# Seven-product FFN on one core: norm in place, down-projection activations moved to the operand tiles, residual loads moved ahead of the last store

## The chip, the core and the metric

The kernel runs on one core of a Trainium2 chip. The metric is the device time of one execution in microseconds, the median of several runs. Five engines work side by side, each through its own queue in order: TensorE (PE, matmuls; its weight loads are listed as PEld), VectorE (DVE), ScalarE (ACT), GpSimd (POOL) and SyncE (SP, which here issues most of the DMAs). They pass work on through semaphores. Matmul results land in PSUM; everything else lies in SBUF.

## The reference, cut to what matters

The program is two residual layers on a 1024 x 1024 float32 stream x (tokens by features): a state-space mixer (ssd), a gated conv feed-forward block (FFN), differential attention (attn), and a second FFN. The change is in the FFN and in the hand-over into it:

```python
def conv_ffn(xn, up_w, conv_w, conv_b, down_w):      # D_MODEL 1024, D_FF 2816, FFN_CONV 3
    h = causal_dwconv(xn @ up_w, conv_w, conv_b)     # up: 1024 -> 2 * 2816
    a, b = h[..., :D_FF], h[..., D_FF:]
    return (silu(a) * b) @ down_w                    # down: 2816 -> 1024

x = x + conv_ffn(rmsnorm(x, norm_ffn_g), ...)
```

## The kernel before

**Layout and precision.** Features lie on the 128 partitions, tokens on the free axis. The residual is 16 SBUF tiles `xres[m, h]` of 128 x 512 floats (8 feature blocks m, 2 token halves h; in a trace `x`). Every float32 operand of a product is split in a high part (cast by ACT) and a low part (subtracted by DVE or POOL), and a product is three matmuls, high·high, high·low and low·high, each 128 x 128 by 128 x 512. `parts` (L805 to L808) splits activations, `split_weight` (L99 to L107) and `split` (L895 to L907) split weights: cast on ACT, low part on POOL (`wh`, `wl`).

**Norm (L205 to L252).** The mixer that ends before an FFN adds its result into `xres` and feeds squares to a `Norm`. `stats` turns the sums into a reciprocal root per token and copies it to a small tile `rkeep`; `apply` spreads it over a PSUM tile (`token_spread`, L185 to L194: small DVE products `dg`, then matmuls `rb`), scales x into a scratch tile `xnt` (L245), and splits that into `xn_h`, `xn_l` (`xh`, `xl` in a trace). x itself keeps the residual.

**Up half of an FFN (L788 to L962).** Weight blocks 0 to 3 (`PLAIN = 2` pairs) are multiplied in the plain way: 4 blocks x 2 halves x 24 matmuls = 192 (L860 to L870). The other 20 pairs of blocks go through a seven-product scheme (L933 to L961): a pair's weights and the normalised x are 2 x 2 quarters; with four sums of weight quarters (`sums`, L909 to L918) and four sums of x quarters (T1 to T4), seven products of 12 matmuls each, 84 a pair, stand for eight. PSUM tiles of a pair are `px`, `py`, `pz`, `pw`; ACT copies px out three times and DVE adds py, pz and pw. `pz` is used twice in a pair: the fourth product (pz<-t1) fills it, DVE reads it at L953, then the last product (pz<-xh) fills it again, and DVE adds that at L957.

`combine` (L831 to L855) makes T1 to T3 while the plain blocks run: it spreads both halves' roots again (4 `dg`, two `rb`), stores the residual to DRAM (`xm_d`, 16 DMAs), scales x again into `cv` scratch (16 products, L843), makes 16 differences (L847, L850, L852, L855) and splits them. The last difference goes into the tile of x, and T4 is split from it (L871 to L873).

`conv` (L810 to L826) runs once a pair: ACT applies the last tap, DVE the other two (L817), ACT the silu, DVE the product (L822), SP the store to DRAM (`a_d`). Pair 0's result is split on the chip instead (`pre`).

**Down half (L966 to L1018).** After the last pair the x tiles are allocated anew and loaded from `xm_d` (L966, the DMAs at L357). The 22 pairs are summed in groups, `FFN_GROUPS` = (0,1) (1,5) (5,9) (9,13) (13,16) (16,19) (19,22). `fetch` loads a group's stored results (`ad`) and splits them into `ah`, `al`, tiles of a pool of their own; `down` runs 48 wide matmuls per pair of blocks into `dp` (L118 to L120), and DVE adds each `dp` into x (L1002).

**What sets the order.** The framework's scheduler places instructions in each engine's queue by the program's order and by the memory that pools give back; DMAs of the residual and of `a_d` share SP's queue. `up.close()` and `wp.release()` (L961, L962) give back the memory of the up half.

## Time and profile before

| | us |
|---|---|
| median of 3 runs (lowest, highest) | 3100.83 (3097.57, 3105.54) |
| profiled execution, its own time | 3096.0 |
| its span, first to last instruction | 3094.3 |
| ssd, from 0 | to 877 |
| first FFN | 877 to 1612 |
| attention | to 2341 |
| second FFN | to 3094 |

| whole span | PE | PEld | DVE | ACT | POOL |
|---|---|---|---|---|---|
| busy us | 2866.7 | 2217.7 | 2117.1 | 1240.1 | 1334.3 |
| share | 93% | 72% | 68% | 40% | 43% |

The mean granted TensorE clock is 0.966 of full speed. A matmul's time in a row is from its start to its end in the pipeline, and matmuls overlap; what one costs is the distance from its start to the next start. In rows of waits, "PE px L924 <- ACT wh L903" is idle time of PE before matmuls into px that ended with ACT's cast of wh.

### The profile page before, as it was taken

How to read it: one execution, taken by the hardware profiler on the slowest of the kernel's cores; microseconds unless marked ns; L12 is line 12 of the kernel's file. 1: busy time of each engine (PE TensorE's matmuls, PEld its weight loads, DVE VectorE, ACT ScalarE, POOL GpSimd, SP SyncE). 2: the span in 40 equal slices, each digit the busy share in tenths (PEclk: the TensorE clock that was granted, in tenths of full speed). 3: DMA queues.
4: the chain of work that ended last, by engine and by line, in shares of the span. 5: the costliest groups of instructions: out<-in, count | busy, mean ns of one | idle time of the engine just before them, and what ended most of it. 6: DMA issues, size and time to landing. Idle time of an engine off the chain costs nothing.

```text
span 3094.3 us, 36239 instructions
## 1 busy us (share of the span) xinstructions
PE 2866.7 (93%) x13164; PEld 2217.7 (72%) x13164; DVE 2117.1 (68%) x3244; ACT 1240.1 (40%) x1973; POOL 1334.3 (43%) x892
## 2 busy tenths in 40 slices
PE   6999999989987999979998999999998799998999
PEld 4877777767775777767876666666676577776887
DVE  4646666677788777763357888888769877776333
ACT  4444444443334444432124555545444444443111
POOL 2245555547455444421235333333436544442222
PEclk8999999999998999989999999999999899999999
DMA  3445554555422222133332112111633222213323
GB/s 95 139 128 166 154 165 149 174 184 173 138 99 75 82 82 82 69 123 109 99 106 78 50 55 62 55 55 49 194 113 104 75 82 82 82 68 136 103 92 113
DMA packets 182979, 327.85 MB, mean 106 GB/s; under 512 B 20432, under 2 KB 88016, under 8 KB 182800
## 3 DMA queue, kind: packets, MB, share of 16 engines
q1 hardware_dynamic: 155536, 251.07, 24.7%
q10 hardware_dynamic: 18432, 58.73, 5.7%
q0 software_dynamic: 8832, 15.73, 2.1%
q8 instruction: 104, 1.70, 0.2%
q14 instruction: 75, 0.61, 0.1%
HBM read 240.99 MB, written 76.09 MB: 102 GB/s over the span
## 4 chain that ended last, share of the span: by engine, by line
PE 46%; DVE 32%; POOL 6%; issue 6%; ACT 5%; DMA 4%; SPq 0%; ACTq 0%; DVEq 0%; POOLq 0%
PE mm L293 6%; PE mm L294 6%; PE mm L295 6%; DVE cv L817 6%; PE dp L119 5%; PE dp L120 5%; PE dp L118 5%; PE pz L924 4%; DVE cv L822 4%; DVE sa L915 3%; POOL wl L904 3%; PE s L1310 2%; DVE cv L442 2%; DVE dg L190 1%; PE s L1309 1%
## 5 line engine op out<-in xcount | busy, mean ns | idle before, releaser
L105 POOL TENSOR_TENSOR wl<-ws,wh 128x1024 fp32r<-128x1024 f32 (+3 forms) x208 | 449.6, 2162 | 809.7 <-ACT wh L103 731.8
L293 PE MATMUL mm<-xh,wh 128*128 128x512 f32 x1280 | 543.7, 425 | 11.9 <-ACT xh L246 9.7
L294 PE MATMUL mm<-xl,wh 128*128 128x512 f32 x1280 | 510.7, 399 | 2.4 <-DVE xl L247 1.7
L295 PE MATMUL mm<-xh,wl 128*128 128x512 f32 x1280 | 510.3, 399 | 1.3 <-POOL wl L105 1.3
L103 ACT CAST wh<-ws 128x1024 fp32r<-128x1024 f32 (+3 forms) x208 | 192.5, 926 | 457.8 <-PE dp L119 248.8
L1002 DVE TENSOR_TENSOR x<-x,dp 128x512 f32<-128x512 f32 x224 | 151.9, 685 | 261.2 <-PE dp L120 247.9
L293 PEld LDWEIGHTS mm<-xh,wh 128*128 128x128 f32 x1280 | 247.7, 194 | 76.4 <-issue 18.1
L294 PEld LDWEIGHTS mm<-xl,wh 128*128 128x128 f32 x1280 | 247.1, 193 | 57.8 <-issue 8.4
L295 PEld LDWEIGHTS mm<-xh,wl 128*128 128x128 f32 x1280 | 245.6, 192 | 56.6 <-POOL wl L105 2.0
L119 PE MATMUL dp<-al,wh 128*128 128x512 f32 x672 | 266.0, 396 | 2.0 <-DVE al L808 1.8
L118 PE MATMUL dp<-ah,wh 128*128 128x512 f32 x672 | 264.3, 396 | 1.4 <-ACT ah L807 1.4
L120 PE MATMUL dp<-ah,wl 128*128 128x512 f32 x672 | 265.5, 395 | 0.0
L817 DVE SCALAR_TENSOR_TENSOR cv<-raw,fcw,cv 128x1024 f32<-128x1024 f32 x176 | 230.1, 1367 | 5.6 <-ACT cv L815 5.5
L442 DVE SCALAR_TENSOR_TENSOR cv<-raw,cw,cv 128x1024 f32<-128x1024 f32 x72 | 126.2, 1754 | 55.2 <-ACT cv L440 28.2
L1324 ACT ACTIVATE p<-s,nb,rq 128x256 f32<-128x256 f32 (+7 forms) x128 | 107.0, 836 | 114.9 <-DVE nb L1313 61.2
L119 PEld LDWEIGHTS dp<-al,wh 128*128 128x128 f32 x672 | 126.1, 188 | 33.9 <-DVE al L808 3.6
L118 PEld LDWEIGHTS dp<-ah,wh 128*128 128x128 f32 x672 | 125.9, 188 | 33.7 <-ACT ah L807 2.8
L120 PEld LDWEIGHTS dp<-ah,wl 128*128 128x128 f32 x672 | 126.1, 188 | 30.5
L904 POOL TENSOR_TENSOR wl<-sa,wh 128x1024 fp32r<-128x1024 f32 x40 | 97.3, 2434 | 109.3 <-ACT wh L903 104.6
L904 POOL TENSOR_TENSOR wl<-sc,wh 128x1024 fp32r<-128x1024 f32 x40 | 127.9, 3198 | 6.6 <-ACT wh L903 6.1
L904 POOL TENSOR_TENSOR wl<-ws,wh 128x1024 fp32r<-128x1024 f32 x40 | 103.6, 2590 | 29.9 <-ACT wh L903 29.9
L822 DVE TENSOR_TENSOR cv<-cv 128x1024 f32<-128x1024 f32 x44 | 114.8, 2610 | 0.4
(330 smaller groups left out, 6667.4 us busy)
## 6 DMA issues: line engine op xcount, KB each, us to landing
ws<-in_ffn_up_w_dram SPq DMA_DIRECT2D x96, 512.0 KB
a_d<-cv SPq DMA_DIRECT2D x42, 512.0 KB
ad<-a_d SPq DMA_DIRECT2D x42, 512.0 KB
ws<-in_ssd_in_w_dram ACTq DMA_DIRECT2D x40, 512.0 KB
seg<-acs_d SPq DMA_DIRECT2D x32, 512.0 KB
ws<-in_ssd_out_w_dram ACTq DMA_DIRECT2D x32, 512.0 KB
xbc_d<-cv SPq DMA_DIRECT2D x24, 512.0 KB
xc<-xbc_d SPq DMA_DIRECT2D x32, 384.0 KB
```

The costliest lines, as they stand in the source:

```text
L103: act.copy(wh[:, :n], ws[:, :n])
L105: pool.tensor_tensor(wl[:, :n], ws[:, :n], wh[:, :n], op=ALU.subtract)
L118: pe.matmul(ps, wh[:, m, k, :], xh, start=k == 0, stop=False)
L119: pe.matmul(ps, wh[:, m, k, :], xl, start=False, stop=False)
L120: pe.matmul(ps, wl[:, m, k, :], xh, start=False, stop=k == n - 1)
L293: pe.matmul(ps, wh[:, 0, k, :], xh, start=k == 0, stop=False)
L294: pe.matmul(ps, wh[:, 0, k, :], xl, start=False, stop=False)
L295: pe.matmul(ps, wl[:, 0, k, :], xh, start=False, stop=k == nk - 1)
L442: dve.scalar_tensor_tensor(cv, raw[:, 1 + k:1 + k + T], cw[:, i, k:k + 1], cv, op0=ALU.mult, op1=ALU.add)
L817: dve.scalar_tensor_tensor(cv, raws[b][:, 2 + k:2 + k + T], cw[:, n, k:k + 1], cv, op0=ALU.mult, op1=ALU.add)
L822: dve.tensor_tensor(cvs[1], cvs[0], cvs[1], op=ALU.mult)
L904: pool.tensor_tensor(wl, t, wh, op=ALU.subtract)
```

## The change

- **Norm in place.** `apply(in_place=True)` writes the scaled x into x itself, in all four hand-overs into an FFN (two per layer). The residual is stored to `xm_d` by the mixers, as each block is finished. `stats` no longer copies to `rkeep`.
- **Combine.** x now holds the normalised values, so the second spread of the roots and the 16 scalings go. Four differences per quarter block stay, in place. T1's low part is POOL's, T2's DVE's, T3's DVE's for even k and POOL's for odd (before: POOL's).
- **Starts.** The first seven-product pair's weights are loaded ahead of the last plain block; its a1 split stands ahead of the sums; conv 0 stands after plain block (1, 2), conv 1 in the first pair. The two pools of the weight buffers are swapped between odd and even pairs.
- **One bank by ScalarE.** ACT copies pz after its first product; DVE adds px to the copy, and reads pz no more in the middle of a pair.
- **Down half.** The split activations of a group of up to 4 pairs lie in the tiles `xh`, `xl` of the operand; groups are (0,4) (4,8) (8,12) (12,16) (16,19) (19,22), and no pair stays on the chip. Group 0 is fetched inside the last pair. The 16 x loads stand directly behind the pairs; the last pair's conv, with its store, comes after the first four tiles of the down half.
- **Pads.** 24 floats per partition are left free ahead of the FFN's tiles, and `cbm` of the ssd has two buffers instead of one.

```diff
-            self.r = nrm.tile([P, 4], F32, name="rkeep", tag="rkeep", bufs=4)
-            dve.tensor_copy(self.r, r)
...
-                t = nrm.tile([P, HT], F32, name="xnt", tag=tag, bufs=2 if tag == "sq" else 1)
+                t = x if in_place else nrm.tile([P, HT], F32, name="xnt", tag=tag, bufs=2 if tag == "sq" else 1)
...
+                    store_x(xm_d[0], m, h)
...
+        s1.tile([P, FFN_PAD], F32, name="fpad")
...
-            r0 = token_spread(lambda shape, name: ups.tile(shape, F32, name=name, tag="z"), n0.r)
-            r1 = token_spread(lambda shape, name: ups.tile(shape, F32, name=name, tag="w"), n1.r)
...
-                scaled(t0, k, 0)
-                scaled(t1, k, 1)
-                dve.tensor_tensor(t0, t1, t0, op=ALU.subtract)
-                parts(t0, T1[0][:, k], T1[1][:, k], False)
-                scaled(u1, HB + k, 1)
...
+                a0, a1, b0, b1 = xres[k, 0], xres[k, 1], xres[HB + k, 0], xres[HB + k, 1]
+                dve.tensor_tensor(a0, a1, a0, op=ALU.subtract)
+                parts(a0, T1[0][:, k], T1[1][:, k], False)
+                dve.tensor_tensor(a1, b1, a1, op=ALU.subtract)
+                dve.tensor_tensor(b1, b1, a0, op=ALU.subtract)
+                parts(b1, T2[0][:, k], T2[1][:, k], True)
+                parts(a1, T3[0][:, k], T3[1][:, k], k % 2 == 0)
+                dve.tensor_tensor(b0, b0, b1, op=ALU.subtract)
...
+                acts[gi] = [xnp.tile([P, KB, HT], F32R, name=f"a{c}{gi}", tag=f"x{c}{gi % 2}") for c in "hl"]
...
             product(pz, cur["a2"][1], Q[0], True)
+            act.copy(half(hi, 1), pz)
...
             product(px, cur["a3"][0], Q[2], False)
             act.copy(half(hi, 0), px)
+            dve.tensor_tensor(half(hi, 1), half(hi, 1), px, op=ALU.add)
...
-            dve.tensor_tensor(half(hi, 1), half(hi, 0), pz, op=ALU.add)
...
-        open_x(xm_d, (0, 1))
+        open_x(None, (0, 1), False)
+        for m in range(KB):
+            for h in range(2):
+                sp.dma_start(xres[m, h], xm_d[i][m * P:(m + 1) * P, h * HT:(h + 1) * HT])
...
+                    if (gi, mp) == (0, 0):
+                        conv(PAIRS - 1, (lo, hi))
```

How the queues stand, at three places. On DVE, in the first FFN where combine starts, before (`rsh`, `rsl` are the parts of a root, `cv` is scratch, `x0_0` is block 0, half 0):

```order
L190 TENSOR_TENSOR dg0_7135<-ident_79,rsh_7130 128x512
L190 TENSOR_TENSOR dg1_7138<-ident_79,rsl_7132 128x512
L190 TENSOR_TENSOR dg0_7146<-ident_79,rsh_7141 128x512
L190 TENSOR_TENSOR dg1_7149<-ident_79,rsl_7143 128x512
L843 SCALAR_TENSOR_TENSOR cv_7168<-x0_0_92,norm_ffn_g_86,rb_7134 128x512
L843 SCALAR_TENSOR_TENSOR cv_7168<-x0_1_100,norm_ffn_g_86,rb_7145 128x512
L843 SCALAR_TENSOR_TENSOR cv_7169<-x4_1_104,norm_ffn_g_86,rb_7145 128x512
L847 TENSOR_TENSOR cv_7168<-cv_7168 128x512
```

and on DVE at the same place now:

```order
L246 TENSOR_TENSOR xl1_7051<-x6_1_108,xh1_7050 128x512
L831 TENSOR_TENSOR x0_0_94<-x0_1_102,x0_0_94 128x512
L831 TENSOR_TENSOR x1_0_95<-x1_1_103,x1_0_95 128x512
L833 TENSOR_TENSOR x0_1_102<-x4_1_106,x0_1_102 128x512
L833 TENSOR_TENSOR x1_1_103<-x5_1_107,x1_1_103 128x512
L834 TENSOR_TENSOR x4_1_106<-x4_1_106,x0_0_94 128x512
L834 TENSOR_TENSOR x5_1_107<-x5_1_107,x1_0_95 128x512
```

The differences now follow the last low part of the norm directly, with no spread and no scaling between. On DVE, in a pair in the middle of the up half, from a weight sum to the last addition, before:

```order
L916 TENSOR_TENSOR sc_7658<-ws_7586,ws_7588 128x512
L917 TENSOR_TENSOR sc_7658<-ws_7586,sa_7657 128x512
L953 TENSOR_TENSOR raw_7592<-raw_7592,pz_7596 128x512
L955 TENSOR_TENSOR raw_7592<-raw_7592,pw_7597 128x512
L957 TENSOR_TENSOR raw_7590<-raw_7590,pz_7596 128x512
```

and now:

```order
L900 TENSOR_TENSOR sc_7589<-ws_7516,ws_7518 128x512
L901 TENSOR_TENSOR sc_7589<-ws_7516,sa_7588 128x512
L951 TENSOR_TENSOR raw_7522<-raw_7522,px_7524 128x512
L955 TENSOR_TENSOR raw_7522<-raw_7522,pw_7527 128x512
L959 TENSOR_TENSOR raw_7520<-raw_7520,pz_7526 128x512
```

The count and the places stay; the first addition reads px instead of pz. On SP, at the end of the first FFN's up half, before:

```order
L826 DMA a_d0_6951<-cv_10028 128x1024
L95 DMA ws_10273<-in_ffn_down_w_dram 128x256
L95 DMA ws_10299<-in_ffn_down_w_dram 128x256
L95 DMA ws_10325<-in_ffn_down_w_dram 128x1024
L826 DMA a_d0_6951<-cv_10146 128x1024
L357 DMA x0_0_10159<-xm_d0_6952 128x512
L357 DMA x1_0_10160<-xm_d0_6952 128x512
```

and now:

```order
L823 DMA a_d0_6956<-cv_9976 128x1024
L920 DMA ad_10087<-a_d0_6956 128x1024
L920 DMA ad_10091<-a_d0_6956 128x1024
L96 DMA ws_10302<-in_ffn_down_w_dram 128x1024
L971 DMA x0_0_10114<-xm_d0_89 128x512
L971 DMA x0_1_10122<-xm_d0_89 128x512
...
L971 DMA x7_1_10129<-xm_d0_89 128x512
L823 DMA a_d0_6956<-cv_10216 128x1024
```

The 16 loads of x moved ahead of the last store of `a_d`, and two loads of `ad` stand ahead of them.

## Rows read from the trace of the kernel before

**Rows 1.** Busy time by stretch: pairs of the first up half, one pair.
```profile
core 0: us, PE busy (x) PEld busy (x) DVE busy (x) ACT busy (x) POOL busy (x), PEclk, DMA share, GB/s
950.00:1365.00 415.00, 399.55 (x1692) 316.93 (x1692) 311.20 (x268) 177.95 (x207) 197.20 (x122) 0.99 0.20 74
998.18:1018.13 19.95, 19.64 (x85) 15.63 (x84) 14.82 (x13) 8.66 (x10) 9.58 (x6) 1.00 0.22 78
```

**Rows 2.** The same view: first up half's start, both changes from up to down.
```profile
877.20:962.00 84.80, 58.90 (x232) 45.78 (x231) 79.29 (x89) 36.99 (x53) 50.65 (x27) 0.84 0.22 76
1357.20:1397.40 40.20, 25.32 (x81) 17.47 (x82) 23.79 (x26) 10.34 (x11) 7.56 (x5) 0.75 0.67 234
2824.90:2863.50 38.60, 24.24 (x87) 16.42 (x87) 22.30 (x26) 10.88 (x12) 7.18 (x5) 0.87 0.71 238
```

**Rows 3.** Waits, 860 to 970 us: engine, line, waited for: us, times, longest.
```profile
PE px L924 <- ACT wh L903: 15.1, 1, 15.1
...
PE rb L192 <- DVE dg L190: 6.4, 3, 3.0
...
PE px L924 <- POOL wl L904: 2.8, 1, 2.8
```

**Rows 4.** Timeline of combine, DVE and POOL: start, us, engine, line, operation.
```profile
901.27 2.84 DVE L190 TENSOR_TENSOR dg<-ident,rsl 128x512 fp32r<-128x512 f32 x1
907.13 1.41 DVE L843 SCALAR_TENSOR_TENSOR cv<-x,norm_ffn_g,rb 128x512 f32<-128x512 f32 x2 [0.78 <-PE rb L192]
909.71 0.68 DVE L850 TENSOR_TENSOR cv<-cv 128x512 f32<-128x512 f32 x1
909.87 1.68 POOL L808 TENSOR_TENSOR t1l<-cv,t1h 128x512 fp32r<-128x512 f32 x1 [6.31 <-ACT t1h L807]
910.43 1.67 DVE L852 TENSOR_TENSOR cv<-cv 128x512 f32<-128x512 f32 x1
941.83 1.64 DVE L855 TENSOR_TENSOR x<-cv 128x512 f32<-128x512 f32 x1
```

**Rows 5.** Timeline of PE in one pair: single matmuls.
```profile
998.18 0.39 PE L924 MATMUL px<-xh,wh 128*128 128x512 f32 x1
...
1003.62 0.40 PE L924 MATMUL px<-t2h,wh 128*128 128x512 f32 x1
...
1012.00 0.39 PE L924 MATMUL pw<-xh,a22h 128*128 128x512 f32 x1
...
1014.56 0.40 PE L924 MATMUL pw<-xh,a22l 128*128 128x512 f32 x1
1015.26 0.51 PE L924 MATMUL pz<-xh,wh 128*128 128x512 f32 x1 [0.31 <-DVE raw L953]
1015.61 0.40 PE L924 MATMUL pz<-xl,wh 128*128 128x512 f32 x1
```

**Rows 6.** The same pair by groups: busy us, mean ns | idle before.
```profile
L915 DVE TENSOR_TENSOR sa<-sa,ws 128x512 f32<-128x512 f32 x1 | 2.9, 2893 | 0.0
L916 DVE TENSOR_TENSOR sc<-ws 128x512 f32<-128x512 f32 x1 | 0.7, 677 | 0.0
L950 ACT COPY raw<-px 128x512 f32<-128x512 f32 x1 | 0.6, 588 | 1.9 <-PE px L924 1.9
```

**Rows 7.** Waits, 1350 to 1400 us, at the first change from up to down.
```profile
PE dp L118 <- DVE x L1002: 12.5, 4, 9.7
...
DVE x L1002 <- DMA x<-xm_d: 8.1, 4, 3.9
```

**Rows 8.** Timeline of SP's queue at the same place.
```profile
1365.46 0.33 SPq L826 DMA_DIRECT2D a_d<-cv  x1
1365.88 12.11 SPq L357 DMA_DIRECT2D x<-xm_d  x16
```

**Rows 9.** Timeline of PE in the down half: two matmuls, 84 apart.
```profile
1450.01 0.40 PE L118 MATMUL dp<-ah,wh 128*128 128x512 f32 x1
...
1469.61 0.40 PE L118 MATMUL dp<-ah,wh 128*128 128x512 f32 x1
```

More of the change, by code (lines that the diff above doesn't have):

```diff
@@ L607, in core_tokens @@
             act.copy(btok, pb[:, 0, :])
-            cbm = sb.tile([P, CH], F32, name="cbm", tag="cbm", bufs=1)
+            cbm = sb.tile([P, CH], F32, name="cbm", tag="cbm")
             dve.tensor_tensor(cbm, pb[:, 1, :], tu, op=ALU.mult)
@@ L858, in ffn_layer, with load_pair @@
+        def load_pair(j):
+            p = wp if j % 2 else wpool
+            ws = []
+            for b in range(2):
+                t = p.tile([P, 1024], F32, name="ws", tag="ws", bufs=2)
+                sp.dma_start(t, a["ffn_up_w"][i, 2 * j + b])
+                ws.append(t)
+            return {"ws": ws}
         raws = [new_raw() for _ in range(2 * PLAIN)]
-        pending = tail[0]
         for h in range(2):
@@ L870, in ffn_layer @@
                     combine()
+                if (h, n) == (1, 2):
+                    conv(0, raws[0:2])
         T4 = [xn_h[1], xn_l[1]]
@@ L874, in ffn_layer @@
         close_x()
-        pre = tc.alloc_tile_pool(name=f"pre{i}", bufs=1, side="right", reuse_waits="tile")
-        xpools.append(pre)
-        acts[0] = tuple(pre.tile([P, T], F32R, name=f"pre{c}", tag=f"pre{c}") for c in "hl")
+        adp = tc.alloc_tile_pool(name=f"ffa{i}", bufs=2, side="right", reuse_waits="tile")
         wp = tc.alloc_tile_pool(name=f"wino{i}", bufs=1, side="right", reuse_waits="tile")
+        xpools.append(adp)
         def quarters(th, tl, k0):
@@ L886, in ffn_layer @@
         Q = [quarters(t[0], t[1], 0) for t in (T1, T2, T3, T4)]
-        def load_pair(j):
-            p, bufs = (wpool, 2) if j % 2 else (wp, 2)
-            ws = []
-            for b in range(2):
-                t = p.tile([P, 1024], F32, name="ws", tag="ws", bufs=bufs)
-                sp.dma_start(t, a["ffn_up_w"][i, 2 * j + b])
-                ws.append(t)
-            return {"ws": ws}
         def split(t, own=False):
@@ L925, in product, with fetch @@
                               skip_group_check=not first)
-        cur = load_pair(PLAIN)
+        acts = {}
+        def fetch(gi, js=None):
+            j0, j1 = FFN_GROUPS[gi]
+            if gi not in acts:
+                acts[gi] = [xnp.tile([P, KB, HT], F32R, name=f"a{c}{gi}", tag=f"x{c}{gi % 2}") for c in "hl"]
+            for j in range(j0, j1) if js is None else js:
+                t = adp.tile([P, 2, HT], F32, name="ad", tag="ad")
+                sp.dma_start(t, a_d[j].rearrange("p (h t) -> p h t", h=2))
+                o = slice(2 * (j - j0), 2 * (j - j0) + 2)
+                parts(t, acts[gi][0][:, o, :], acts[gi][1][:, o, :], True)
+        cur["a1"] = split(cur["ws"][0])
         sums(cur)
-        cur["a1"] = split(cur["ws"][0])
         cur["a2"] = split(cur["sa"])
-        for j in range(PLAIN):
-            conv(j, raws[2 * j:2 * j + 2])
         for j in range(PLAIN, PAIRS):
-            nxt = load_pair(j + 1) if j + 1 < PAIRS else None
+            end = j == PAIRS - 1
+            nxt = None if end else load_pair(j + 1)
             lo, hi = new_raw(), new_raw()
@@ L944, in ffn_layer @@
             act.copy(half(lo, 1), px)
+            if end:
+                fetch(0, (0, 1))
             product(pz, cur["a2"][1], Q[0], True)
+            act.copy(half(hi, 1), pz)
             cur["a4"] = split(cur["ws"][1][:, W2:], True)
@@ L959, in ffn_layer @@
                 nxt["a2"] = split(nxt["sa"])
-            conv(j, (lo, hi))
+                conv(j, (lo, hi))
             cur = nxt
@@ L963, in ffn_layer @@
         up.close()
-        open_x(xm_d, (0, 1))
-        ds = st.enter_context(tc.tile_pool(name=f"ffd{i}", bufs=2, reuse_waits="tile"))
+        open_x(None, (0, 1), False)
+        for m in range(KB):
+            for h in range(2):
+                sp.dma_start(xres[m, h], xm_d[i][m * P:(m + 1) * P, h * HT:(h + 1) * HT])
         dps = st.enter_context(tc.tile_pool(name=f"dps{i}", bufs=4, space=PSUM, reuse_waits="tile"))
-        def fetch(gi):
-            for j in range(*FFN_GROUPS[gi]):
-                if j not in acts:
-                    t = ds.tile([P, T], F32, name="ad", tag="ad")
-                    sp.dma_start(t, a_d[j])
-                    acts[j] = tuple(ds.tile([P, T], F32R, name=f"a{c}", tag=f"a{c}", bufs=6) for c in "hl")
-                    parts(t, acts[j][0], acts[j][1], True)
         offs = {}
@@ L996, in down @@
                         for h in hs:
[L997 to L998 removed]
+                            xs = [(ah[:, 2 * k + h, :], al[:, 2 * k + h, :]) for k in range(kg)]
                             ps = dps.tile([P, HT], F32, name="dp", tag="dp")
@@ L1432, in attn_layer @@
         core.close()
-        (tail.append(norms[1]), head.__setitem__(0, norms[0]))
+        tail.append(norms[1])
     stages = stages or ("ssd", "ffn0", "attn", "ffn1")
     x_d = dram.tile([D, T], F32, name="x_d")
+    xm_d = [dram.tile([D, T], F32, name=f"xm_d{i}") for i in range(DEPTH)]
     open_x(a["x"], (0, 1), False)
```

56 lines of the change are left out of this document (20 added, 36 removed).

## The prediction

> **What bounds the kernel now.** I read busy time by stretch first. In the middle of the first up half PE is busy for 399.55 of 415.00 us [rows 1], at the full clock or nearly (0.99): the products bound the FFN, and no other engine is near, since in the one pair shown DVE has 14.82 of 19.95 us and ACT and POOL under 10. So what a change can win in an FFN is of three kinds: stretches in which PE stands still, the same small wait in every pair, and the distance from one matmul to the next. The change leaves ssd and attention alone but for their last steps, and its number of matmuls is the same apart from two spreads of a root. I therefore look for lost PE time in four places, each of which occurs in both FFNs.
>
> The start of the up half loses most. Between 877.20 and 962.00 us lie 222 wide matmuls by the code: 192 plain ones, the first 24 of the first pair, 6 of spreads. At 0.2267 us each (the distance found below) they need 50.3 of 84.80 us, so 34.5 us are lost, part of it as half-speed clock (PEclk 0.84) [rows 2]. The named waits there are 15.1 us for ACT's cast of the first pair's weights, 6.4 for the spread's DVE products and 2.8 for POOL's low part of weights [rows 3]. The change from up to down loses 40.20 - 81 x 0.2325 = 21.4 us in the first layer and 38.60 - 87 x 0.2325 = 18.4 in the second, 39.8 together [rows 2]; DVE's addition into x is what PE waits for (12.5 us), and it waits for the loads of x (8.1 us) [rows 7]. In a pair PE waits once for DVE's reading of pz, in the order of half a microsecond [rows 5]. And matmuls follow each other at two paces, below.
>
> **The change part by part.** All savings are for both layers, against the profiled execution's own time of 3096.0 us.
>
> *Start of the up half.* Removed are, per layer, four dg products, up to 2.84 us each, with the wait for rb behind them, and 16 scalings of 1.41 / 2 = 0.70 us, 11.3 us of DVE's queue [rows 4]. The order shows the first difference directly behind the norm; it can start some 7.5 us earlier, at 900 instead of 907.5. What is left on DVE is 16 differences, and 8 low parts of T2 and T4, as before, with two of T3 added. Each costs 0.68 alone, and 1.67 when it lies behind a POOL operation of the same size, which itself takes 1.68: the pair at 909.87 and 910.43 shows it [rows 4]. Walking the new queues by hand with the longer price wherever POOL has an operation in hand, the last difference (before: 941.83 + 1.64 = 943.5) ends near 927. The next thing that is late is no longer combine. The plain blocks then end near 937, held by POOL's low parts of their weights; a1's cast now precedes the sums and follows them without the 15.1 us [rows 3]; a2 comes through DVE's sums, ACT's cast and POOL's low part, and is ready near 949.5. So the first px<-t2 starts there instead of at 962.0: 12.5 us a layer, **25 us**. Upper bound: all but the 2.8 us of a first low part, 34.5 - 2.8 = 31.7 a layer, 63. Lower bound: a2 was last before too, and T3's two low parts on DVE cost 2.9 us each when blocked by a large POOL operation (the price of L915 in [rows 6]), so -6 a layer, -12. I take the walk, which follows both queues to the wait that ends last.
>
> *One bank by ScalarE.* The distance from the last matmul into pw to the first pz<-xh is 0.70, the next one 0.35, where 0.23 is usual: 0.47 + 0.12 = 0.59 us a pair [rows 5], 40 pairs, **24 us**. Afterwards ACT copies pz when the fourth product ends, and 24 matmuls (5.5 us) lie between that and the next use of pz, so the wait has no successor there. The copy costs ACT 0.59 us [rows 6], hidden by its 11 us of idle time in a pair [rows 1]. DVE's addition at L951 waits for px as L953 did for the copy of px, and what stands behind it is the addition of pw; px is free for the next pair after 24 matmuls more. If the place of the wait only moved to px, the term is 0; I see no row for a gain above 24.
>
> *From up to down.* Before, the 16 loads of x are issued from 1365.88 on, directly behind the last store of a_d, and take 12.11 us to issue [rows 8]; that store waits for the last conv, which the changed order moves behind the first four tiles of the down half. The loads now wait for memory and, on SP, for two loads of ad and a down weight. By the queues they can go at some 15 us into the last pair of 19, and group 0's operands are ready within it, since their fetch stands inside the pair. DVE's first addition into x comes 3 us after the first down matmul, and the x loads land in the same order. I leave 2 us a layer: 39.8 - 4 = **36 us**, with 0 as the lower bound (the loads are no earlier in time) and 39.8 as the upper. The conv that is moved costs DVE less than the 14.82 us of a whole pair [rows 1], among the additions of the down half, which have four PSUM tiles of 12 matmuls (11 us) as cover; I cost it at nothing, at most 4 us a layer if the cover falls short.
>
> *Place of the operands.* Products with xh follow each other at (1003.62 - 998.18) / 24 = 0.2267 us, those with T1 to T3 at (1012.00 - 1003.62) / 36 = 0.2328 [rows 5], and those of the down half with ah, al at 19.60 / 84 = 0.2333 [rows 9]. The activations now lie in the tiles of xh and xl: 2 layers x 21 pairs x 48 = 2016 matmuls x (0.2333 - 0.2267) = **13 us**. The bounds are 0, if the place isn't what sets the pace, and, with the T products, whose tiles the 24 floats of pad shift, 2 x 20 x 36 = 1440 matmuls x 0.0062 = 9 more. I take 13 and not 22: xh is seen at the faster pace and the shifted T tiles at none. One rule speaks against this term. The Trainium skill, page "SBUF — State Buffer", section "Who interferes with whom", says "PE and ACT never wait on anyone." By it a matmul's pace could not hang on where its operand lies, the 13 us would be 0 and the sum 85; the two paces, 0.2267 and 0.2333, leave that open, since the loops differ in more than the place.
>
> *At nothing.* The stores of the residual from the mixers: they already stood between the last steps of ssd and attention, and SP's queue has room there. rkeep, two buffers for cbm, the swapped weight pools and conv 0 and 1 moved: DVE and SP operations beside a busy PE, under 1 us each.
>
> Sum: 25 + 24 + 36 + 13 = 98, so 3096.0 - 98 = 2998 for a profiled execution. The median before is 4.8 us above that execution's own time; I add it, 3002.8, and forecast **3003 us**.
>
> **The rivals.**
>
> *The T products gain too* (the pad works as the place does): 9 us more, 2994. For it: T and ah/al show the same slow pace, so one cause may serve both. Against it: nothing in the rows shows which address is fast.
>
> *The place does not matter*: 13 us less, 3016. For it: the two paces come in different loops, and products of other operands may differ for other reasons (how high and low parts alternate, which tile the weights come from). By the sentence of the Trainium skill quoted above this is what would happen.
>
> *The start is no earlier*: combine ends earlier, but PE waits for a2 or for POOL's plain weights until 962 as before, so the wait only changes its name. 25 us less, 3028. For it: POOL's low parts of 1.68 us and DVE's block each other, and the walk rests on that.
>
> *The change does not do what it says*: the loads of x stand ahead of the last store in the queue, but the loads of ad ahead of them wait for a buffer, and x still arrives 10 us late. 36 less, 3039.
>
> *Slower: DVE becomes the bound in the pairs.* Of a pair's four sums one is blocked behind POOL for 2.89 us, the others take 0.68 [rows 6]. The swapped pools and the copy on ACT shift when casts come, and so when POOL starts. If the other three were blocked too, DVE would need 14.82 + 3 x 2.2 = 21.4 us, with the 2.3 us in which it must wait for the last product 23.7, against 19.95 - 0.59 = 19.4 in the forecast: 40 x 4.3 = 172 more, 3175 us. It decides from a pair of 21.9 us on, where 40 x 2.5 eats the 98. Against it: the order leaves DVE's and POOL's rows of a pair as they are but for one operand, and POOL is idle for half of a pair [rows 1].
>
> **How the numbers follow.** A difference of 0.3% (9 us) is about what a measurement of this kernel can tell from none. Chances: forecast (3003) 0.40, T products too (2994) 0.18, place doesn't matter (3016) 0.17, start no earlier (3028) 0.13, loads still late (3039) 0.08, slower (3175) 0.04. The range reaches from 2976, T products with a start 9 us a layer better than walked, to 3045, where two of the middle rivals meet (place and start: 3041); about 2 in 10 is left outside. All cases but the last are faster by over 0.3%; two or three of the losses at once would give no change: faster 0.92, same 0.04, slower 0.04.
>
> **What would show it.** Start: px<-t2 within 73 us of the FFN's first product instead of 85, and the wait on rb gone; wrong if PE's waits before it still add to 25 us. Bank: no wait before pz<-xh, a pair of 19.4 us; wrong if PE waits there for px or DVE passes 19 us in a pair. Up to down: the first dp within 1 us of the last pz, no wait for x over 2 us. Place: dp matmuls at 0.227 us; T products at 0.233 by the forecast and at 0.227 by the first rival. The largest risk is the walk at the start, then the loads of x.

## The result, and the profile after

The changed kernel takes 2995.14 us (median of 4 runs, 2990.09 to 2999.18), the kernel before 3102.56 us beside it (4 runs): a ratio of 0.9655, 95% interval 0.9632 to 0.9677, 107 us or 3.5% less. The forecast was 3003, its range 2976 to 3045. The profiled execution took 2992.0 us against 3096.0, so the traces differ by 104.

The table cuts both traces at the same four instructions of each layer, by the starts of matmuls: the second plain matmul of an FFN (0.2 us behind the first), the first px<-t2, the first dp, the last dp. The ssd row begins with the first matmul of the execution, 7.5 us into the span. "First" and "second" are the two FFNs.

| stretch, us | before | changed | saved | forecast, both layers |
|---|---|---|---|---|
| ssd, to the second plain matmul | 869.8 | 866.9 | 2.9 | 0 |
| start of the up half, first / second | 84.5 / 86.5 | 70.5 / 72.7 | 14.1 / 13.9 | 25 |
| pairs, first / second | 395.6 / 395.9 | 384.0 / 383.9 | 11.5 / 11.9 | 24 |
| down half, first / second | 272.2 / 263.9 | 246.2 / 240.2 | 26.0 / 23.8 | 36 + 13 |
| attention | 713.7 | 714.2 | -0.5 | 0 |

The busy time of the same stretches of the changed kernel, in the columns of [rows 1] (stretch, its us, busy us and count of each engine, granted clock, DMA share, GB/s): the start, seventeen and a half pairs, one pair, and the change from up to down in both layers.

```profile
874.10:944.81 70.71, 55.72 (x228) 43.12 (x226) 64.04 (x65) 35.58 (x50) 44.70 (x24) 0.95 0.26 90
980.00:1320.00 340.00, 340.00 (x1479) 276.52 (x1478) 259.29 (x227) 163.01 (x195) 166.22 (x104) 1.00 0.22 78
1003.00:1022.33 19.33, 19.33 (x86) 15.71 (x85) 14.73 (x13) 9.12 (x12) 9.56 (x7) 1.00 0.23 82
1328.50:1364.20 35.70, 35.32 (x156) 28.73 (x155) 21.46 (x25) 12.70 (x12) 8.16 (x4) 1.00 0.80 282
2745.00:2775.00 30.00, 29.41 (x130) 23.83 (x129) 17.89 (x21) 11.65 (x11) 6.94 (x3) 1.00 0.83 294
```

Against [rows 1, 2] the start is 14 us shorter, PE is busy for all of 340 us of pairs, and the two stretches in which PE did 81 and 87 matmuls in about 40 us are filled: 156 matmuls in 35.7 us, 130 in 30.0, at the full clock where it was 0.75 and 0.87. DVE has 14.73 us in a pair, as before (14.82): the rival in which it becomes the bound did not come.

The waits of PE at the start that answer to [rows 3] (engine, line, what was waited for, us in all, times, longest):

```profile
PE mm L121 <- POOL wl L106: 6.7, 3, 2.8
...
PE px L908 <- ACT raw L934: 3.9, 1, 3.9
```

The 15.1 us for the cast of a1 are gone, and the spreads of combine with their 6.4. What is late now is POOL's low part of the plain weights, and a2: the 3.9 us before px<-t2 are put down to ACT's copy of px, which stood on ACT behind a2's cast and a step of a conv, and that cast had waited 2.4 us for DVE's weight sums. DVE's first and last difference of combine (start, us):

```profile
895.03 3.48 DVE L831 TENSOR_TENSOR x<-x,x 128x512 f32<-128x512 f32 x2
...
922.47 0.69 DVE L837 TENSOR_TENSOR x<-x,x 128x512 f32<-128x512 f32 x1
```

The walk had them begin at 900 and end near 927; they began at 895 and ended at 923, where the kernel before ended at 943.5 [rows 4]. The FFN itself starts 3.1 us earlier now (874.13 against 877.22), so counted from its first product the walk was closer still: it had 23 us for the beginning, 50 for the end and 72.3 for the first px<-t2, and the trace has 21, 49 and 70.7. The matmuls of one pair, as in [rows 5]:

```profile
1019.49 0.39 PE L908 MATMUL px<-xh,wh 128*128 128x512 f32 x1
...
1024.93 0.40 PE L908 MATMUL px<-t2h,wh 128*128 128x512 f32 x1
...
1033.31 0.39 PE L908 MATMUL pw<-xh,a22h 128*128 128x512 f32 x1
...
1038.81 0.39 PE L908 MATMUL px<-xh,wh 128*128 128x512 f32 x1
```

A pair is 1038.81 - 1019.49 = 19.32 us, where 19.4 was forecast. The products with xh keep 5.44 / 24 = 0.2267 us, those with T operands 8.38 / 36 = 0.2328: as before, although the pads have moved them. No wait stands before pz<-xh:

```profile
1016.53 0.40 PE L908 MATMUL pw<-xh,a22l 128*128 128x512 f32 x1
1016.77 0.39 PE L908 MATMUL pz<-xh,wh 128*128 128x512 f32 x1
```

In the down half the distance is (1420.76 - 1400.36) / 90 = 0.2267 us, where [rows 9] had 0.2333:

```profile
1400.36 0.39 PE L119 MATMUL dp<-ah,wh 128*128 128x512 f32 x1
...
1420.76 0.39 PE L119 MATMUL dp<-ah,wh 128*128 128x512 f32 x1
```

And SP's queue at the change from up to down, for [rows 8]: the 16 loads of x are issued 2 us before the first dp (1328.82), and DVE's first addition comes at 1336.55 without a wait for them.

```profile
1322.72 3.67 SPq L920 DMA_DIRECT2D ad<-a_d  x2
...
1326.96 12.21 SPq L971 DMA_DIRECT2D x<-xm_d  x16
1341.38 0.32 SPq L823 DMA_DIRECT2D a_d<-cv  x1
```

### The profile page after: what moved, and what is told of

Same layout as the page of the kernel before. It is cut to its first block, busy times and chain, and to the rows that moved or that the text cites. A ratio compares the mean times of both kernels' runs of the same rounds, so it can differ in the third digit from the quotient of the medians.

```text
span 2990.2 us, 36019 instructions
## 1 busy us (share of the span) xinstructions
PE 2822.9 (94%) x13156; PEld 2211.7 (74%) x13156; DVE 2069.7 (69%) x3160; ACT 1257.2 (42%) x2005; POOL 1320.9 (44%) x880
## 5 line engine op out<-in xcount | busy, mean ns | idle before, releaser
L106 POOL TENSOR_TENSOR wl<-ws,wh 128x1024 fp32r<-128x1024 f32 (+2 forms) x200 | 444.7, 2223 | 769.4 <-ACT wh L104 719.8
L104 ACT CAST wh<-ws 128x1024 fp32r<-128x1024 f32 (+2 forms) x200 | 191.0, 956 | 440.6 <-PE dp L120 222.5
L997 DVE TENSOR_TENSOR x<-x,dp 128x512 f32<-128x512 f32 x192 | 130.3, 684 | 211.3 <-PE dp L121 210.9
L120 PE MATMUL dp<-al,wh 128*128 128x512 f32 x704 | 274.7, 390 | 1.0 <-DVE al L808 1.0
L119 PE MATMUL dp<-ah,wh 128*128 128x512 f32 x704 | 274.8, 390 | 0.0
L121 PE MATMUL dp<-ah,wl 128*128 128x512 f32 x704 | 274.6, 390 | 0.0
L817 DVE SCALAR_TENSOR_TENSOR cv<-raw,fcw,cv 128x1024 f32<-128x1024 f32 x176 | 232.3, 1375 | 12.7 <-ACT cv L815 12.6
L120 PEld LDWEIGHTS dp<-al,wh 128*128 128x128 f32 x704 | 132.6, 188 | 29.2 <-DVE al L808 1.8
L119 PEld LDWEIGHTS dp<-ah,wh 128*128 128x128 f32 x704 | 132.6, 188 | 28.0 <-DVE raw L955 0.6
L121 PEld LDWEIGHTS dp<-ah,wl 128*128 128x128 f32 x704 | 132.5, 188 | 27.5
```

The costliest lines, as they stand in the source:

```text
L104: act.copy(wh[:, :n], ws[:, :n])
L106: pool.tensor_tensor(wl[:, :n], ws[:, :n], wh[:, :n], op=ALU.subtract)
L119: pe.matmul(ps, wh[:, m, k, :], xh, start=k == 0, stop=False)
L120: pe.matmul(ps, wh[:, m, k, :], xl, start=False, stop=False)
L121: pe.matmul(ps, wl[:, m, k, :], xh, start=False, stop=k == n - 1)
L817: dve.scalar_tensor_tensor(cv, raws[b][:, 2 + k:2 + k + T], cw[:, n, k:k + 1], cv, op0=ALU.mult, op1=ALU.add)
```

## The experiments

The theory is the prediction's: four savings with one cause each. Most experiments undo one cause, or measure it by itself; where an edit undoes more, the text says so. The profiles of kernels that leave attention untouched differ there by up to 8 us (713 to 721), which I could not explain, and the total of a variant moves with it; so effects of a few us are read from the stretch that a variant touches, and each total is given with its interval.

### The pace of matmuls: where the operand lies

A kernel of matmuls alone, 48 for each place.

```diff
+    for n in range(21):
+        run(f"x{(X0 + 8192 * n) // 1024}", X0 + 8192 * n, W0)
+    for n in range(16):
+        wa = W0 + 12288 * n
+        run(f"w{wa // 1024}", X0 if n != 1 and n != 2 else X0 + 32768, wa)
+    for b, nm in ((X0, "l"), (X0 + 102400, "m")):
+        for s in (32, 64, 96):
+            run(f"{nm}{s}", b + s, W0)
+    for s in (32, 64, 96):
+        run(f"v{s}", X0, W0 + s)
```

> Nothing of the layers is computed and the output is a copy of x: only matmuls in the order high-high, high-low, low-high, 48 for each place, with no other engine at work. The 16 KB of the moving operand lie at 21 places, 8 KB apart, from 42 KB to 218 KB of the partition, with the weights at 26 KB; then the weights lie at 16 places, 12 KB apart, with the moving operand at 42 KB; then both are shifted by 32, 64 and 96 bytes. Theory (the place of the operand sets the pace): 0.2267 us from one matmul to the next below about 108 KB, 0.233 above 121 KB. Rival one (offset within 128 bytes): the pace changes only with the shifts. Rival two (traffic of other engines, or the form of the loop, sets the pace): 0.2267 at every place.

PE's timeline of it, one row for all cases of a letter (start, us, count): x is the moving operand at 21 places, w the weights at 16, l and m the operand shifted by 32, 64 and 96 bytes at two places, v the weights shifted.

```profile
30.98 228.19 PE L113 MATMUL x<-big 128*128 128x512 f32 x1006
259.01 174.24 PE L113 MATMUL w<-big 128*128 128x512 f32 x768
433.08 33.57 PE L113 MATMUL l<-big 128*128 128x512 f32 x144
466.50 33.57 PE L113 MATMUL m<-big 128*128 128x512 f32 x144
499.91 33.79 PE L113 MATMUL v<-big 128*128 128x512 f32 x144
```

From start to start, x took (259.01 - 30.98) / 1006 = 0.2267 us a matmul, w 0.2267: the place in the partition is nothing, from 42 to 218 KB. l and m took 0.2321 and v 0.2335: a shift by less than 128 bytes costs what the T operands cost. My theory of a region of the partition fell. But the first rival does not fit either: in the program's memory layout the weight tiles and xh, the fast pair, both start 96 bytes past a multiple of 128, and so do the T tiles of the changed kernel, which are slow. (The addresses are those that the framework gives the tiles when it builds the kernels.) So I formed another: what counts is the distance between the two addresses.

```diff
+    for nm, dx, dw in (("aa", 0, 0), ("ab", 64, 0), ("ac", 128, 0), ("ad", 256, 0), ("ae", 384, 0), ("af", 512, 0),
+                       ("ag", 1024, 0), ("ba", 0, 64), ("bb", 0, 128), ("bc", 0, 256), ("bd", 0, 384), ("be", 0, 1024),
+                       ("ca", 32, 32), ("cb", 64, 64), ("cc", 96, 96), ("cd", 128, 128), ("ce", 256, 256)):
+        run(nm, X0 + dx, W0 + dw, 8)
```

> Nothing of the layers is computed and the output is a copy of x: 96 matmuls for each case, weights and moving operand shifted by themselves and together. The first places study gave 0.2267 us at every place of the partition, and 0.232 to 0.2335 when one operand alone was shifted by 32, 64 or 96 bytes. Theory (the distance between the weights' and the operand's address sets the pace, taken modulo 256 or more, since the shifted T tiles lie 128 bytes off and are slow): operand shifted alone by 64 or 128 slow, by 512 and 1024 fast, 256 tells the period; both shifted together by any amount fast. Rival (each operand must start at a multiple of 128 bytes by itself): 128, 256, 384, 512 fast, both shifted by 32, 64 or 96 slow.

The same view, a row for each case of 96 matmuls:

```profile
52.54 22.15 PE L113 MATMUL ab<-big 128*128 128x512 f32 x96
74.53 22.48 PE L113 MATMUL ac<-big 128*128 128x512 f32 x96
96.85 21.97 PE L113 MATMUL ad<-big 128*128 128x512 f32 x96
118.66 22.55 PE L113 MATMUL ae<-big 128*128 128x512 f32 x96
141.05 21.94 PE L113 MATMUL af<-big 128*128 128x512 f32 x96
162.82 21.92 PE L113 MATMUL ag<-big 128*128 128x512 f32 x96
184.58 22.56 PE L113 MATMUL ba<-big 128*128 128x512 f32 x96
206.98 22.48 PE L113 MATMUL bb<-big 128*128 128x512 f32 x96
229.30 21.94 PE L113 MATMUL bc<-big 128*128 128x512 f32 x96
251.07 22.48 PE L113 MATMUL bd<-big 128*128 128x512 f32 x96
...
338.78 21.96 PE L113 MATMUL cc<-big 128*128 128x512 f32 x96
360.57 21.95 PE L113 MATMUL cd<-big 128*128 128x512 f32 x96
```

The distance from one row's start to the next, over 96: operand shifted by 64 bytes 0.2291 us, by 128 0.2325, by 256 0.2272, by 384 0.2332, by 512 0.2268; weights shifted by 64 0.2333, by 128 0.2325, by 256 0.2268; both shifted together by 96 bytes 0.2270, and in the four other cases of that kind no more than 0.2271. So it is the distance that matters, and of the distances tried the multiples of 256 bytes are fast and all others slow, by different amounts. By the layouts, distance to the weight tile modulo 256: xh 0, activations of the changed kernel 0 (fast); T and ah, al before 32, T after 128, the a22 weights against xh 128, all slow (0.232 to 0.233). The pad of 96 bytes moved the T tiles from one slow distance to another. The Trainium skill, page "SBUF — State Buffer", section "Who interferes with whom", says "PE and ACT never wait on anyone"; in this kernel of matmuls alone no other engine worked, so the two paces do not contradict it, but neither does it say when PE is slower by itself. The prediction took that sentence to rule out that the place of an operand counts, and that reading failed.

In the changed kernel, the activations of every second group moved to where T1 and T2 lay, 128 bytes off:

```diff
-                acts[gi] = [xnp.tile([P, KB, HT], F32R, name=f"a{c}{gi}", tag=f"x{c}{gi % 2}") for c in "hl"]
+                q, tg = (dsp[0], "a") if gi % 2 else (xnp, "x")
+                acts[gi] = [q.tile([P, KB, HT], F32R, name=f"a{c}{gi}", tag=f"{tg}{c}{gi % 2}") for c in "hl"]
```

> The changed kernel, with the split activations of every second group of the down half in a pool of their own at 146 to 179 KB, where T1 and T2 lay; the even groups stay in the operand's tiles. Theory (place): the 1056 matmuls of the odd groups take 0.233 us each instead of 0.227, the even ones stay at 0.227, 7 us more in all, about 3002 us. Rival (one tile of eight blocks for a group, instead of a tile for each pair, made the pace): all groups at 0.227, 2995 us.

PE's timeline, two matmuls 84 apart in an odd group, and two 87 apart in an even one:

```profile
1385.53 0.40 PE L119 MATMUL dp<-ah,wh 128*128 128x512 f32 x1
...
1405.13 0.40 PE L119 MATMUL dp<-ah,wh 128*128 128x512 f32 x1
...
1430.02 0.39 PE L119 MATMUL dp<-ah,wh 128*128 128x512 f32 x1
...
1449.74 0.39 PE L119 MATMUL dp<-ah,wh 128*128 128x512 f32 x1
```

19.60 / 84 = 0.2333 in the odd group, 19.72 / 87 = 0.2267 in the even one, same loop, same tile form. The down halves took 249.9 and 243.8 us, 3.7 and 3.6 more than in the changed kernel: 7.3 for half of the matmuls, as expected. In total 2999.49 us, ratio 0.9678 (0.9660 to 0.9696). So of the 49.8 us that both down halves saved, 13 to 15 are the pace.

### One bank copied by ScalarE

```diff
-            act.copy(half(hi, 1), pz)
...
-            dve.tensor_tensor(half(hi, 1), half(hi, 1), px, op=ALU.add)
+            dve.tensor_tensor(half(hi, 1), half(hi, 0), pz, op=ALU.add)
```

> The changed kernel with one part undone: VectorE reads pz again in the middle of a pair, ScalarE copies it no more. Theory: the wait before the first pz<-xh comes back, 0.59 us x 40 pairs, 24 us more than the changed kernel, about 3019 us, and a pair takes 19.8 instead of 19.2 us. Rival (the pairs became shorter by the other order of weight pools and casts): the same time as the changed kernel, 2995 us.

3022.63 us, ratio 0.9750 (0.9734 to 0.9767). The pairs took 396.4 and 396.5 us, 12.4 and 12.6 more than in the changed kernel, 24.9 together, and the wait is the old one:

```profile
1018.92 0.39 PE L908 MATMUL pw<-xh,a22l 128*128 128x512 f32 x1
1019.62 0.50 PE L908 MATMUL pz<-xh,wh 128*128 128x512 f32 x1 [0.32 <-DVE raw L950]
```

The copy alone makes the pairs' saving; the swapped pools, which stayed in place here, have no part in it.

### From up to down

First the last pair's conv back inside the pair:

```diff
-                conv(j, (lo, hi))
+            conv(j, (lo, hi))
...
-                    if (gi, mp) == (0, 0):
-                        conv(PAIRS - 1, (lo, hi))
```

> The changed kernel with the last pair's conv and its store back inside the pair, ahead of the loads of x. Theory (the loads of x waited behind that store): x comes 8 us or more later, and PE, which has four tiles of the down half (11 us) to run on, stands still for 2 to 10 us in each layer: 3000 to 3015 us. Rival (the first group of four pairs gives enough cover by itself, the place of the store is nothing): 2995 us, no wait for x over 1 us.

3002.83 us, ratio 0.9686 (0.9669 to 0.9702); the down halves took 247.9 and 240.4 us, 1.7 and 0.2 more. PE waited for no x. But the experiment did not make x late either. SP's queue:

```profile
1330.48 10.57 SPq L971 DMA_DIRECT2D x<-xm_d  x15
1344.49 0.32 SPq L823 DMA_DIRECT2D a_d<-cv  x1
1344.91 0.37 SPq L971 DMA_DIRECT2D x<-xm_d  x1
```

The scheduler still put 15 of the 16 loads ahead of the store. What had held them before is then not the order in the code. The memory differs: in the old layout the first x tiles lay over the conv's scratch (`cv`), so they had to wait for the store that read it; in the new one the scratch pool stands ahead of T1 to T3 and the first x tiles lie over T3. This move of the scratch pool is part of the change, but it stands neither in the list of the change nor in the prediction. So the scratch pool was put back behind T1 to T3, to be given back with them, and the groups of four were left:

```diff
-        sb = st.enter_context(tc.tile_pool(name=f"ffu{i}", bufs=2, reuse_waits="tile"))
         tp = up.enter_context(tc.tile_pool(name=f"fft{i}", bufs=1, reuse_waits="tile"))
+        sb = up.enter_context(tc.tile_pool(name=f"ffu{i}", bufs=2, reuse_waits="tile"))
```

(with the edit above)

> The changed kernel with the last pair's conv back in the pair, and the conv's scratch tiles placed behind T1 to T3 and given back with them, as in the kernel before, so that the first loads of x wait for the last store of the conv. The groups of four pairs stay. Theory (the memory held the loads back, and the stall was long because the first group of one pair gave no cover): loads of x issued some 8 us after the last product, 11 us of the down half to run on meanwhile, PE waits 2 to 4 us a layer, about 5 us more than the changed kernel. Rival (late loads cost what they cost before, whatever the group): 10 to 18 us a layer, 3015 to 3030 us.

3024.92 us, ratio 0.9760 (0.9745 to 0.9774); the down halves took 260.5 and 257.0 us, 14.3 and 16.8 more than in the changed kernel, 31 together. SP's queue and the waits (1325 to 1380 us):

```profile
1343.55 0.32 SPq L823 DMA_DIRECT2D a_d<-cv  x1
...
1347.27 10.74 SPq L971 DMA_DIRECT2D x<-xm_d  x16
```

```profile
PE dp L119 <- DVE x L997: 10.7, 1, 10.7
```

All 16 loads now stand behind the store, and PE waits 10.7 us for the first addition. After that wait it runs a while at the lower clock: the granted clock is 0.85 over 1328 to 1373, and the first matmuls follow each other at 0.43 us instead of 0.2267. The conv's place in the code is the same as in the experiment above, and only the place of the pools in memory differs, so that place was the cause. So the rival came: late loads cost 14 to 17 us a layer also with a first group of four pairs. My price was too low, since the loads came not 8 but 17 us after the last product (the first dp starts at 1330.23): the conv's store is issued 13 us after it, because splits of the next activations stand between the conv's steps on DVE, and between that store and the loads SP still has a load of ad and a down weight, 3.4 us. The two edits account for 31 of the some 36 us that the two changes from up to down saved, 29 of them the memory's; the rest (4 to 6) is left to the larger first group and the fetch inside the pair, which were not tried apart.

### The start of the up half

The norm and the sums as in the kernel before, everything else as in the changed one (but the T3 parts are back on POOL, and cbm has one buffer):

```diff
-            for k in range(HB):
-                a0, a1, b0, b1 = xres[k, 0], xres[k, 1], xres[HB + k, 0], xres[HB + k, 1]
-                dve.tensor_tensor(a0, a1, a0, op=ALU.subtract)
...
+            r0 = token_spread(lambda shape, name: ups.tile(shape, F32, name=name, tag="z"), n0.r)
+            r1 = token_spread(lambda shape, name: ups.tile(shape, F32, name=name, tag="w"), n1.r)
+            for k in range(HB):
+                ta, tb = (sb.tile([P, T], F32, name="cv", tag="cv") for _ in range(2))
...
+                scaled(t0, k, 0)
+                scaled(t1, k, 1)
+                dve.tensor_tensor(t0, t1, t0, op=ALU.subtract)
```

> The changed kernel with the norm written to scratch again and the sums of x made as before, from the residual scaled a second time, with the second spread of the roots; the earlier a1 split, conv 0 and conv 1 stay where the change put them; one buffer for cbm. Theory (the queue of VectorE at the start of the up half set the 14 us): the waits for the spread come back (6 us a layer) and the T sums end 15 us later; but a1 no longer waits for conv 0, so of the 28 us gained at both starts 15 to 25 are lost. Rival (the order of a1 and conv 0 made the gain): under 6 us lost.

3030.88 us, ratio 0.9780 (0.9764 to 0.9796). The starts took 82.0 and 83.7 us, 11.5 and 11.0 more, and the pairs 5.5 and 4.5 more. Up to the third px<-t2 of a layer the loss is 12.5 and 10.5 us, 23 in all, within the 15 to 25 expected: 23 of the start's 28 us. The rest of the pairs' loss is not the start's: PE stands still for 4.0 us in the first layer and 4.4 in the second between the last product and the first dp, where the changed kernel has no such wait. It waits there for DVE's last addition of the pair; why the edit delays that, at the other end of the up half, was not tried. PE's waits, 870 to 975 us and 1320 to 1360 us:

```profile
PE pw L924 <- ACT a22h L903: 10.2, 1, 10.2
PE rb L193 <- DVE dg L191: 6.1, 3, 2.9
...
PE dp L119 <- DVE raw L975: 4.0, 1, 4.0
```

The spread's 6 us are back, and a 10 us wait stands at the fourth weight quarter. ACT's cast of a1 is as early as in the changed kernel:

```profile
935.29 1.05 ACT L903 CAST wh<-ws 128x1024 fp32r<-128x1024 f32 x1
```

That is 57 us behind the FFN's first product, where the changed kernel has 55.5 and the kernel before 71.9. So the 15.1 us wait for that cast is gone here too, and yet most of the gain is lost, because PE then waits for the fourth quarter: an early a1 by itself is worth 5 us of the 28 at most. Then the order of the start undone, with the norm in place (and without pad and second cbm buffer):

```diff
-                if (h, n) == (1, 2 * PLAIN - 1):
-                    cur = load_pair(PLAIN)
...
-                if (h, n) == (1, 2):
-                    conv(0, raws[0:2])
...
-        cur["a1"] = split(cur["ws"][0])
+        cur = load_pair(PLAIN)
         sums(cur)
+        cur["a1"] = split(cur["ws"][0])
         cur["a2"] = split(cur["sa"])
+        for j in range(PLAIN):
+            conv(j, raws[2 * j:2 * j + 2])
```

> The changed kernel with the norm in place kept, and the order of the start undone: the first pair's weights loaded after the plain blocks, sums ahead of the a1 split, conv 0 and conv 1 behind the a2 split; the 24 floats of pad and the second buffer for cbm are undone too, which other stretches show. Theory (the length of VectorE's queue made most of the start's 28 us, the order the rest): 3 to 8 us a layer later at the start, that is 6 to 16 in all. Rival (the order alone is enough for PE's 15 us wait): 12 us a layer or more. For the pad: by the period of 256 bytes the T products stay at 0.233 us, since 128 bytes off and 32 bytes off are both slow, so nothing. For cbm: ssd ends 3 us later, as in the kernel before.

2999.14 us, ratio 0.9686 (0.9667 to 0.9704). The starts took 70.4 and 72.8 us: no change at all, and both the theory and the rival miss. The trace shows why: from conv 0's silu to the first copy of px, ACT has the same operations in the same order as in the changed kernel, with a1's cast ahead of the splits of T4, and so have DVE and POOL over that time. The scheduler made the same queues from the other order of the code. So the experiment shows that the order of the code is worth nothing here; what another order of the queues would cost with the norm in place, no run shows. The T products stayed at 0.233 us, so the pad is nothing. ssd ended at 869.0 us against 866.9; the three traces with one buffer for cbm have 869.0 to 871.0, the nine with two 866.7 to 868.8, so about 2 us, near the spread; two of the three also lack the norm in place, so that the buffer makes these 2 us is not shown.

### Versions that go further

If the distance sets the pace, T1 to T3 and a22 can be moved to a fast one:

```diff
-FFN_PAD = 24
+FFN_PAD = 120
...
+        adp.tile([P, 32], F32, name="apad", tag="apad", bufs=1)
```

> The changed kernel with T1 to T3 moved by 384 bytes and the fourth weight quarter (a22) by 128, so that all operands and weights of a product lie a multiple of 512 bytes apart. Theory (the distance of the addresses sets the pace): the 1440 matmuls with T operands go from 0.233 to 0.227 us, the 480 with a22 from 0.232 to 0.227, 9 + 2 = 11 us less than the changed kernel, 191.0 instead of 192.0 tenths of a us in a pair becoming 18.9 to 19.05 us. Rival (T products are slow for another reason, such as their order with the sums): no difference.

2992.82 us, ratio 0.9652 (0.9637 to 0.9667): not told apart from the changed kernel. The pace came as expected, from px<-t2 to px<-t3 24 matmuls in 5.44 us, 0.2267; but the pairs took 381.6 us, 2.4 less a layer and not 5.6 (a steady pair 19.22 us), for the next thing was late:

```profile
1005.09 0.39 PE L909 MATMUL px<-t2h,wh 128*128 128x512 f32 x1
...
1010.53 0.39 PE L909 MATMUL px<-t3h,wh 128*128 128x512 f32 x1
...
1011.03 0.50 PE L909 MATMUL px<-t3h,wl 128*128 128x512 f32 x1
```

The third matmul takes the low part of a3, which POOL ends only at 1010.97, since it stood for 4.4 us before a small clearing that waits for DVE's conv:

```profile
1007.64 0.10 POOL L800 MEMSET raw<- 128x4 f32 x1 [4.43 <-DVE cv L817]
1007.75 3.22 POOL L889 TENSOR_TENSOR wl<-sc,wh 128x1024 fp32r<-128x1024 f32 x1
```

Two of the kernels above bear both points out without having been built for it. In the one with the old place of the scratch pool and in the one with the norm apart, the T tiles happen to lie a multiple of 256 bytes from the weights: px<-t2 and pz<-t1 run at 0.2267 to 0.2269 there on average, but PE waits inside px<-t3 as here, and their pairs stay at 19.3 to 19.4 us.

So the clearing was taken out of the pairs:

```diff
+        ring = [sb.tile([P, T + 4], F32, name=f"raw{q}", tag=f"raw{q}", bufs=1) for q in range(4)]
+        for t in ring:
+            pool.memset(t[:, 0:4], 0.0)
...
-            raw = sb.tile([P, T + 4], F32, name="raw", tag="raw", bufs=4)
-            pool.memset(raw[:, 0:4], 0.0)
-            return raw
+            ring.append(ring.pop(0))
+            return ring[-1]
```

> The aligned kernel (operands and weights of a product a multiple of 512 bytes apart) with four fixed tiles for raw, whose first columns GpSimd clears once per layer instead of twice in a pair. In the aligned kernel GpSimd waits 4.4 us a pair with such a clearing for VectorE's conv, and the low part of a3 behind it is late: PE waits before the third matmul of px<-t3. Theory: that low part starts 1.6 us earlier, the wait goes, a pair takes 84 x 0.2267 = 19.05 us and the pairs of a layer 378 us instead of 381.6, so 7 us less than the aligned kernel and 12 less than the changed one. Rival (VectorE and GpSimd block each other, so that the low part takes as much longer as it starts earlier): 381.6 as before.

2999.87 us, ratio 0.9686 (0.9666 to 0.9705): not better, and the pairs of a layer took 386.1 us. In the first layer 11 pairs take 19.04 us, the 84 x 0.2267 that matmuls alone need, and 7 take 20.0: there PE waits for ACT's copy of px, which stands behind a silu that waits for DVE (990 to 1300 us).

```profile
ACT cv L823 <- DVE cv L820: 37.5, 16, 3.6
...
PE px L912 <- ACT raw L943: 4.6, 7, 0.7
```

Last, the silu tied behind that copy, by a bias column read from it, beside the changed kernel once more:

```diff
+                    z = sb.tile([P, 1], F32, name="z", tag="z")
+                    act.activation(z, after[:, 0:1], AF.Identity, scale=0.0)
+                    act.activation(cvs[0], cvs[0], AF.Silu, bias=z)
...
+                fin(half(lo, 1))
```

> The aligned kernel with the four fixed raw tiles, and the conv's silu tied behind ScalarE's copy of px after the third product, by a bias column that is read from that copy and scaled to zero. In the kernel with the fixed tiles half of the pairs took 19.04 us and half 20.0, with PE waiting for that copy, which stood on ScalarE behind a silu that waited for VectorE. Theory: all pairs at 19.04 us, the pairs of a layer 378 us against 384 in the changed kernel, 12 us less in all, about 0.4% under it. Rival (VectorE, whose product of the conv now comes later, hands the wait on to the additions and the sums): pairs of 19.5 us or more.

> The changed kernel itself, unaltered, beside the last version on the same chip: 0.9655 of the kernel before by every theory, pairs of 19.33 us, attention 714 us or, as in some of the variants, up to 721.

2989.74 us, ratio 0.9657 (0.9643 to 0.9671), and the changed kernel 2994.27, ratio 0.9674 (0.9659 to 0.9689): the intervals overlap, so it is not shown to be faster. Its steady pairs take 19.19 us, all of them, against 19.33 to 19.39 in the changed kernel beside it, but not 19.04: the two bias columns, 32 bytes each, moved the T tiles by 64 bytes, and their products run at 0.229 to 0.2305, near the 0.2291 of case ab above. The product with a22 behind them lies at a fast distance but takes 0.231 on average, and only its last two matmuls of 12 come at 0.227. So the slower pace outlasted the T products by ten matmuls, which the layout alone does not say; in the aligned kernel it outlasted PE's small wait in px<-t3 by some five. No version here beats the changed kernel beyond doubt.

## Why the prediction was right, point by point

- **Start, 25 us; measured 28.** The walk along DVE's and POOL's queues gave the right size and the right places (within 2 us at each step, counted from the FFN's first product), and 23 of the 28 are lost again without the norm in place. One part of the reason fell: I let a1's place ahead of the sums share in the gain. With the old norm an early a1 saves 5 us at most, and with the new norm the old order of the code gives the same queues.
- **Bank, 24 us; measured 23.5**, 24.9 when undone, at the named instruction.
- **From up to down, 36 us, and place, 13 us; measured 49.8 together**, of which the place is 13 to 15 (the pace in the rows, and the odd groups). What I called the place is the distance to the weights: the tiles xh and xl are fast because they lie a multiple of 256 bytes from them. The 36 came, but the step "that store waits for the last conv, which the changed order moves" named the wrong cause: with the conv moved back the stall stays away; with the old memory layout as well, 31 us of it return. That the loads were early enough was right, but by luck: the scratch pool's move, which freed their memory, was not in my working. They were issued 17.5 us into the last pair, where I had some 15. I read a queue (the loads stood behind a store) as the reason for the loads' place in it, and did not ask which memory they were to be written to.
- **T products: no gain, as forecast**, though for no reason that I had, so by luck. The pad changes their distance to the weights from 32 to 128 bytes (modulo 256), and both are slow.
- **The rival that the place doesn't matter** fell with the odd groups of the down half at 0.2333, in the same loop as the even ones at 0.2267, though the place in the partition by itself is indeed nothing; **the rival that the T products gain too** with 0.2328.
- **What was missed**: about 2 us in ssd, perhaps by the second buffer for cbm, which is not shown. Of the 6 us between the 98 forecast and the 104 by which the traces differ, 3 are the start's and 2.4 ssd and attention together; the remaining 2 us from 3003 to 2995.14 are within the spread of the runs.

## What to carry to other kernels

Where a load stands late in a queue, look at the memory it is to be written to before the order of the code: here tiles that lay over another pool's scratch waited for the last reader of that scratch, and that cost 29 us, while two changes of order in the code left the queues as they were, or nearly so. Look at the queues that come out before you call an edit of the order an experiment. Walk the one queue that ends last, operation by operation with measured prices, to the next wait that takes its place: it gave the start of both layers within 3 us. And when a loop runs at its engine's pace, compare the distance between instructions for different operands; 3% lay in the addresses.

## What the runs showed of the hardware

With no other engine at work, full clock, and matmuls of 128 x 128 by 128 x 512 with a new weight load for each, the distance between two matmuls was 0.2267 us where the addresses of weights and moving operand lay a multiple of 256 bytes apart (0.2272 at most), and 0.229 to 0.2335 where they did not: with the operand shifted 0.2291 for 64 bytes, 0.2325 for 128, 0.2332 for 384; with the weights shifted 0.2333 for 64. Shifting both together cost nothing (0.2271 at most), and neither did any place in the partition from 26 to 218 KB. In the last versions five to ten matmuls at a fast distance, behind a slower product or a small wait, still came at 0.23 us before the pace was 0.227 again. I had not expected that the distance of two tiles could set PE's pace, nor that a bias column of 32 bytes in a pool ahead of them could take half of that gain away. Why it is so, no run here shows.
